# Second mixer: 35 elementwise instructions (product of y and gate, two running sums) moved from VectorE to GpSimd

## Chip, cores and metric

The kernel runs on one core of one Trainium2 chip. The metric is the device time of one execution in microseconds (us), lower is better. A profiled execution also gives a span, which is the time from its first to its last instruction.

## What is computed

The reference is two transformer-like blocks, one after the other, on 512 tokens of width 1024, in fp32. The change touches only the mixer of the second block, a convolution branch and a Mamba-2 branch (SSD):

```
u = a_half * sigmoid(b_half)
u = causal_depthwise_conv(u, conv_dw_w, conv_dw_b)      # 31 taps, 1024 channels
u = silu(layer_norm(u, conv_ln_w, conv_ln_b))           # mean and variance over the channels
...
y = ssd_chunked_scan(...) + d_skip * xs
y = y * silu(z)                                         # product of y and gate
yg = y.reshape(b, L, N_GROUPS, D_INNER // N_GROUPS)     # 4 groups of 512 channels
yg = yg * rsqrt(mean(yg * yg, axis=-1) + eps)           # sum of squares over a group
```

## The kernel before

Channels lie on the 128 partitions and the 512 tokens on the free axis, so that a tile is 128x512. A projection (`proj`) is 24 matmuls of 128x512 from weight blocks; every fp32 weight block is split into a high part by ScalarE (`whi`, line 201) and a low part by VectorE (`wlo`, line 203). The work is written as generators: `group_in` projects one group's tiles and, between projections, `pump` takes the next piece of two background queues. One holds the convolution (`conv31`, then `conv_sums`), the other the SSD of the group before (`ssd`). A scheduler then fixes one order for each engine; at run time every engine takes its instructions strictly in that order and waits on semaphores.

`conv31` makes 8 tiles of channels `co`, each by 30 multiply-adds on VectorE (line 1996, both tensor inputs in SBUF), and adds each finished tile to `self.sum` (`csum`, lines 2000 and 2002, seven adds). `conv_sums` starts with a matmul of `csum` (`pmean`, line 2025).

`ssd(g)` runs four times. Its last phase is a loop over i = 0 to 3, one tile of 128 channels each: TensorE makes `pyd` and `pyo` (line 2171), VectorE combines them into y (lines 2251, 2252, 2253), multiplies y by the gate z (line 2254), ScalarE squares y (lines 2257 and 2259), and VectorE adds the square into `ss` (tile `gsum`, line 2260; for i = 0 the square itself begins the sum). After the loop `col_sums` sums `gsum` over partitions with four small matmuls (`pms`, line 2010), VectorE scales them (`rg`, line 2016), GpSimd takes the power -1/2 (line 2017), and TensorE spreads the result over the partitions (`spread`, line 371), which VectorE multiplies into y (line 2270).

`decays` brings the decay tile `E` from DRAM by a transfer that GpSimd issues (line 2193). There are four `E` buffers, so the transfers of group g+1 are issued when the `pyd` matmuls of group g have freed them; they stand in GpSimd's queue between the end phases' steps. ScalarE's first operation on an `E` tile is line 2201.

Of the kernel before, what the change touches and what calls it, by code (L numbers as in the profile page):

```python
# [12 lines left out]
ALU = mybir.AluOpType  # L13
# [1903 lines left out]
class Mixer2:  # L1917
# [67 lines left out]
    def conv31(self):  # L1985

        K, nc = self.K, self.K.nc
        V, A = nc.vector, nc.scalar
        self.co = []
        self.sum = K.u(name="csum")  # L1990
        for i in range(8):
            u, c = self.uc[i], K.u(name="co")
            w = lambda j: K.cols["dw", j * 8 + i]
            A.activation(c, u[:, 0:512], AF.Identity, scale=w(0), bias=K.cols["db"][:, i:i + 1])
            for j in range(1, 31):
                V.scalar_tensor_tensor(c, u[:, j:j + 512], w(j), c, op0=ALU.mult, op1=ALU.add)  # L1996
                if j % 4 == 0:
                    yield
            if i == 1:
                V.tensor_tensor(self.sum, self.co[0], c, op=ALU.add)  # L2000
            elif i:
                V.tensor_tensor(self.sum, self.sum, c, op=ALU.add)
            self.co.append(c)
            yield

# [155 lines left out]
    def ssd(self, g, tiles):  # L2161

        K, nc = self.K, self.K.nc
        V, A, Te = nc.vector, nc.scalar, nc.tensor
        B, C, X, Z = tiles[0], tiles[1], tiles[2:6], tiles[6:10]
        ch = lambda x, c: x[:, c * 128:(c + 1) * 128]
        hs = slice(8 * g, 8 * g + 8)
        h8 = lambda x: x.rearrange("p (h j) -> p h j", j=64)
        bc = lambda x, c: x[:, c, hs, None].to_broadcast([128, 8, 64])
        def mul(*args, **kw):  # L2170
            self.line(lambda: Te.matmul(*args, start=True, stop=True, **kw))

        def turn(out, x):
            self.line(lambda: Te.transpose(out, x, K.ident))


        pbt = K.pt([128, 3, 128], name="pbt")
        for c in range(3):
            turn(pbt[:, c], ch(B, c))
        bt = K.u([128, 3, 128], name="btok")  # L2180
        A.activation(bt, pbt, AF.Copy)
        pcb = K.pt([128, 4, 128], name="pcb")
        for c in range(4):
            mul(pcb[:, c], ch(B, c), ch(C, c))
        cb = K.u([128, 4, 128], name="cbm")
        V.tensor_tensor(cb, pcb, self.tri[:, None, :].to_broadcast([128, 4, 128]), op=ALU.mult)
        Es, eas = [], []

        def decays(i):
            h0 = 8 * g + 2 * i  # L2190
            E = K.v4([128, 2, 4, 128], name="E")
            E2 = E.rearrange("p h c t -> p h (c t)")
            nc.gpsimd.dma_start(E2, self.acd[None, h0:h0 + 2, :].to_broadcast([128, 2, 512]))
            ea = K.u(name="ea")
            for hh in range(2):
                s = slice(hh * 64, hh * 64 + 64)
                A.activation(ea[s, 128:], E2[s, hh, 128:], AF.Exp)
            for hh in range(2):
                for c in range(4):
                    h = 2 * i + hh  # L2200
                    A.activation(E[:, hh, c], E[:, hh, c], AF.Relu, scale=-1.0,
                                 bias=self.acs[:, c, 8 * g + h:8 * g + h + 1])
            A.activation(E, E, AF.Exp, scale=-1.0)
            V.tensor_tensor(E, E, cb[:, None].to_broadcast([128, 2, 4, 128]), op=ALU.mult)
            Es.append(E)
            eas.append(ea)

        yield
        ps = [K.pt(name="pxT") for _ in range(4)]
        for c in range(4):  # L2210
            for i in range(4):
                turn(ps[c][:, i * 128:(i + 1) * 128], ch(X[i], c))
        xd, xws = [], []
        for c in range(4):
            x = K.u(name="xdt")
            V.tensor_tensor(h8(x), h8(ps[c]), bc(self.dt, c), op=ALU.mult)
            xd.append(x)
        for c in range(3):
            xw = K.u(name="xw")
            V.tensor_tensor(h8(xw), h8(xd[c]), bc(self.wd, c), op=ALU.mult)  # L2220
            xws.append(xw)
        decays(0)
        yield
        ps = [K.pt(name="pst") for _ in range(3)]
        for c in range(3):
            mul(ps[c], bt[:, c], xws[c])
        st = [None]
        for c in range(3):
            sn = K.u(name="st")
            if c == 0:  # L2230
                A.activation(sn, ps[c], AF.Copy)
            else:
                V.tensor_tensor(h8(sn), h8(st[c]), bc(self.et, c), op=ALU.mult)
                V.tensor_tensor(sn, sn, ps[c], op=ALU.add)
            st.append(sn)
        decays(1)
        yield
        for i in range(4):
            E, ea, z = Es[i], eas[i], Z[i]
            pd, po = K.pt(name="pyd"), K.pt(name="pyo")  # L2240

            for c in range(4):
                for hh in range(2):
                    h = 2 * i + hh
                    mul(pd[hh * 64:hh * 64 + 64, c * 128:(c + 1) * 128], xd[c][:, h * 64:h * 64 + 64], E[:, hh, c])
            for c in range(1, 4):
                mul(po[:, c * 128:(c + 1) * 128], st[c][:, i * 128:(i + 1) * 128], ch(C, c))
            if i < 2:
                decays(i + 2)
            y = X[i]  # L2250
            V.scalar_tensor_tensor(y, y, self.dsk[:, 4 * g + i:4 * g + i + 1], pd, op0=ALU.mult, op1=ALU.add)
            V.tensor_tensor(ea[:, 128:], po[:, 128:], ea[:, 128:], op=ALU.mult)
            V.tensor_tensor(y[:, 128:], y[:, 128:], ea[:, 128:], op=ALU.add)
            V.tensor_tensor(y, y, z, op=ALU.mult)
            if i == 0:
                ss = K.u(name="gsum")
                A.activation(ss, y, AF.Square)
            else:
                A.activation(z, y, AF.Square)
                V.tensor_tensor(ss, ss, z, op=ALU.add)  # L2260
            yield

        r = self.rsqrt4(self.rg[:, g], self.col_sums(ss), 512, 1e-6)
        yield
        yield
        rs = K.spread(r)
        for i in range(4):
            y = X[i]
            w = K.cols["sn"][:, 4 * g + i:4 * g + i + 1]
            V.scalar_tensor_tensor(y, y, w, rs, op0=ALU.mult, op1=ALU.mult)  # L2270
            self.y.append(y)
        yield
# [223 lines left out]
```

## Time and profile before

| what | value |
|---|---|
| median of 3 runs | 1889.6 us (1889.45 to 1890.53) |
| the profiled execution's own time | 1887.34 us |
| its span | 1885.6 us |
| TensorE busy | 1779.2 us, 94% of the span |
| VectorE busy | 1369.6 us, 73% |
| ScalarE busy | 943.3 us, 50% |
| GpSimd busy | 137.0 us, 7% |
| mean granted TensorE clock | 0.978 |

Busy shares are averages over stages of different kinds. The second mixer's groups run from about 985 to 1262 us of the span and the rest of its convolution until about 1400 us. PE is TensorE, DVE is VectorE, ACT is ScalarE and POOL is GpSimd. In a timeline row an entry with xN merges N neighbouring instructions.

### The profile page before, as it was taken

The page shows a single profiled execution, that of the slowest core. Times are in us where ns is not written, and L with a number is a line of the kernel's source. Part 1 is how long each engine was busy: PE and PEld are TensorE (multiplying, and loading weights), DVE is VectorE, ACT ScalarE, POOL GpSimd, SP SyncE. Part 2 cuts the span into 40 slices and gives each one's busy share as a digit, 9 for nine tenths or more (in the row PEclk, how much of TensorE's full clock was granted, in tenths as well). Part 3 has the DMA queues.
Part 4 walks back from the last instruction along what each step waited for, and adds up shares of the span by engine and source line. Part 5 has one row for each costly group of instructions (what it writes and reads, how often), then busy time and mean ns, then how long its engine had stood idle before and what let it go on. Part 6 is the DMA issues. An engine that isn't in the chain of part 4 may idle for free. (4 is left out here: it accounts for less than half of the span.)

```text
span 1885.6 us, 27902 instructions
## 1 busy us (share of the span) xinstructions
PE 1779.2 (94%) x10696; PEld 1481.2 (79%) x10696; DVE 1369.6 (73%) x2166; ACT 943.3 (50%) x1568; POOL 137.0 (7%) x247
## 2 busy tenths in 40 slices
PE   6998989998999998699999999999999999999997
PEld 3675878887888887478887777878778988788997
DVE  4888877867899997678969999999766753333324
ACT  5732355455888887442348577552253632223223
POOL 4000020121000000220000000000000100000000
PEclk9998989998999998899999999999999999999999
DMA  8732555535899999854433243344834753333334
GB/s 287 255 103 76 150 171 176 177 135 179 275 354 351 360 363 317 283 73 125 123 90 101 79 124 95 96 133 134 230 94 151 237 183 90 101 101 90 118 108 150
DMA packets 332905, 322.27 MB, mean 171 GB/s; under 512 B 16813, under 2 KB 291791, under 8 KB 332764
## 3 DMA queue, kind: packets, MB, share of 16 engines
q1 hardware_dynamic: 319004, 281.96, 47.7%
q0 software_dynamic: 11520, 35.30, 6.4%
q10 hardware_dynamic: 2240, 3.15, 0.5%
q8 instruction: 86, 1.41, 0.3%
q14 instruction: 55, 0.45, 0.1%
HBM read 299.03 MB, written 21.33 MB: 170 GB/s over the span
## 5 line engine op out<-in xcount | busy, mean ns | idle before, releaser
L201 ACT ACTIVATE whi<-wraw 128x1024 fp32r<-128x1024 f32 (+1 forms) x281 | 293.5, 1045 | 618.9 <-PE pin L237 209.8
L203 DVE TENSOR_TENSOR wlo<-wraw,whi 128x1024 fp32r<-128x1024 f32 (+1 forms) x281 | 337.9, 1203 | 210.9 <-ACT whi L201 208.5
L236 PE MATMUL pin<-hhi,whi 128*128 128x512 f32 (+1 forms) x752 | 306.4, 407 | 10.7 <-ACT sgc L2068 4.9
L238 PE MATMUL pin<-hhi,wlo 128*128 128x512 f32 (+1 forms) x752 | 300.3, 400 | 1.7 <-DVE wlo L203 1.7
L237 PE MATMUL pin<-hlo,whi 128*128 128x512 f32 (+1 forms) x752 | 300.7, 400 | 0.0
L236 PEld LDWEIGHTS pin<-hhi,whi 128*128 128x128 f32 (+1 forms) x752 | 141.3, 188 | 49.5 <-ACT sgc L2068 5.7
L1996 DVE SCALAR_TENSOR_TENSOR co<-uc,cols,co 128x512 f32<-128x512 f32 x240 | 176.9, 746 | 2.7
L238 PEld LDWEIGHTS pin<-hhi,wlo 128*128 128x128 f32 (+1 forms) x752 | 141.2, 188 | 39.0 <-DVE wlo L203 2.6
L237 PEld LDWEIGHTS pin<-hlo,whi 128*128 128x128 f32 (+1 forms) x752 | 141.2, 188 | 35.8 <-issue 2.4
L203 DVE TENSOR_TENSOR mwlo<-mwraw,mwhi 128x1024 fp32r<-128x1024 f32 x129 | 154.2, 1214 | 13.5 <-ACT mwhi L201 12.9
L201 ACT ACTIVATE mwhi<-mwraw 128x1024 fp32r<-128x1024 f32 x129 | 133.2, 1050 | 19.6 <-PE pgu L1723 8.2
L238 PE MATMUL pff<-hhi,wlo 128*128 128x512 f32 x336 | 133.0, 396 | 0.3 <-DVE wlo L203 0.3
L236 PE MATMUL pff<-hhi,whi 128*128 128x512 f32 x336 | 133.0, 396 | 0.0
L237 PE MATMUL pff<-hlo,whi 128*128 128x512 f32 x336 | 132.9, 396 | 0.0
L275 DVE SCALAR_TENSOR_TENSOR acc<-araw,silu,acc 128x1024 f32<-128x1024 f32 x70 | 89.7, 1281 | 29.8 <-DMA araw<-in_w_ada_ffn_dram 15.4
L1723 PE MATMUL pgu<-mwhi,xs 128*128 128x256 f32 x392 | 99.9, 290 | 8.3 <-DVEq L1764 8.2
L453 PE MATMUL pres<-wlo,fhi 128*128 128x256 f32 x352 | 97.4, 277 | 1.5 <-DVE wlo L203 1.5
L452 PE MATMUL pres<-whi,flo 128*128 128x256 f32 x352 | 97.2, 276 | 0.0
L450 PE MATMUL pres<-whi,fhi 128*128 128x256 f32 x352 | 97.2, 276 | 0.0
L1724 PE MATMUL pgu<-mwlo,xs 128*128 128x256 f32 x392 | 97.0, 284 | 0.0
L1723 PEld LDWEIGHTS pgu<-mwhi,xs 128*128 128x128 f32 x392 | 75.5, 193 | 8.8 <-issue 8.3
L1724 PEld LDWEIGHTS pgu<-mwlo,xs 128*128 128x128 f32 x392 | 75.4, 192 | 0.7 <-DVE mwlo L203 0.3
(631 smaller groups left out, 3848.1 us busy)
## 6 DMA issues: line engine op xcount, KB each, us to landing
wraw<-in_w_in_dram SPq DMA_DIRECT2D x98, 512.0 KB, 3.8
mwraw<-in_moe_w_up_dram SPq DMA_DIRECT2D x61, 512.0 KB, 7.2
araw<-in_ada_w_dram SPq DMA_DIRECT2D x48, 512.0 KB, 8.1
wraw<-in_w_ffn_in_dram SPq DMA_DIRECT2D x44, 512.0 KB, 3.7
mwraw<-in_moe_w_down_dram SPq DMA_DIRECT2D x33, 512.0 KB, 6.2
mwraw<-in_moe_w_gate_dram SPq DMA_DIRECT2D x33, 512.0 KB, 7.5
wraw<-in_moe_w_down_dram SPq DMA_DIRECT2D x31, 512.0 KB, 6.1
wraw<-in_moe_w_gate_dram SPq DMA_DIRECT2D x29, 512.0 KB, 5.7
```

The lines of the kernel that those rows point to most:

```text
L201: self.nc.scalar.activation(hi[:, :m], raw[:, :m], AF.Copy)
L203: self.nc.vector.tensor_tensor(lo[:, :m], raw[:, :m], hi[:, :m].bitcast(F32), op=ALU.subtract)
L236: t.matmul(out, lh, rh, start=start, stop=False)
L237: t.matmul(out, lh, rl, start=False, stop=False)
L238: return t.matmul(out, ll, rh, start=False, stop=stop)
L275: V.scalar_tensor_tensor(acc, raw[:, i], cs[:, q:q + 1], acc, op0=ALU.mult, op1=ALU.add)
L450: Te.matmul(o, yh[:, s], hi[:, k], start=(first and k == 0 and t == 0), stop=False, skip_group_check=True)
L452: Te.matmul(o, yl[:, s], hi[:, k], start=False, stop=False, skip_group_check=True)
L453: Te.matmul(o, yh[:, s], lo[:, k], start=False, stop=(last and k == kn - 1), skip_group_check=True)
L1723: Te.matmul(pg[:, j], x, hi[:, k], start=(kh == 0 and k == 0), stop=False)
L1724: Te.matmul(pg[:, j], x, lo[:, k], start=False, stop=(kh == 1 and k == 3))
L1996: V.scalar_tensor_tensor(c, u[:, j:j + 512], w(j), c, op0=ALU.mult, op1=ALU.add)
```

## The change

Three kinds of instruction are issued on GpSimd with the same operands: the product of y and z, the sum of a group's squares, and the sum of the convolution's tiles.

```diff
@@ conv31
             if i == 1:
-                V.tensor_tensor(self.sum, self.co[0], c, op=ALU.add)
+                nc.gpsimd.tensor_tensor(self.sum, self.co[0], c, op=ALU.add)
             elif i:
-                V.tensor_tensor(self.sum, self.sum, c, op=ALU.add)
+                nc.gpsimd.tensor_tensor(self.sum, self.sum, c, op=ALU.add)
@@ ssd
-            V.tensor_tensor(y, y, z, op=ALU.mult)
+
+            nc.gpsimd.tensor_tensor(y, y, z, op=ALU.mult)
             if i == 0:
                 ss = K.u(name="gsum")
                 A.activation(ss, y, AF.Square)
             else:
                 A.activation(z, y, AF.Square)
-                V.tensor_tensor(ss, ss, z, op=ALU.add)
+                nc.gpsimd.tensor_tensor(ss, ss, z, op=ALU.add)
```

The blank line shifts all later lines by one: the product is line 2255 in the changed kernel, the squares are 2258 and 2260, the sum is 2261.

The scheduler also orders the engines anew. On GpSimd, in the stretch from the first group's last phase (the fifth `E` transfer belongs to the second group):

```order
-L2193 DMA E<-acs_rows 128x1024 x8
+L2193 DMA E<-acs_rows 128x1024 x4
+L2000 TENSOR_TENSOR csum<-co 128x512
+L2002 TENSOR_TENSOR csum<-csum,co 128x512
+L2193 DMA E<-acs_rows 128x1024
+L2255 TENSOR_TENSOR xbc<-xbc,z 128x512
+L2193 DMA E<-acs_rows 128x1024
+L2255 TENSOR_TENSOR xbc<-xbc,z 128x512
+L2261 TENSOR_TENSOR gsum<-gsum,z 128x512
+L2193 DMA E<-acs_rows 128x1024
+L2255 TENSOR_TENSOR xbc<-xbc,z 128x512
+L2261 TENSOR_TENSOR gsum<-gsum,z 128x512
```

The transfers of the next group's `E`, which stood together, now alternate with the products (`xbc` is y) and the sums of the group that is ending.

On VectorE, at the end of the first group, from the last tile's line 2251 to the scaling of the column sums:

```order
 L2251 SCALAR_TENSOR_TENSOR xbc<-xbc,dsk,pyd 128x512
-L2260 TENSOR_TENSOR gsum<-gsum,z 128x512
 L2252 TENSOR_TENSOR ea<-pyo,ea 128x384
 L203 TENSOR_TENSOR wlo<-wraw,whi 128x1024
 L2253 TENSOR_TENSOR xbc<-xbc,ea 128x384
-L1996 SCALAR_TENSOR_TENSOR co<-uc,cols_11934,co 128x512
-L2254 TENSOR_TENSOR xbc<-xbc,z 128x512
-L1996 SCALAR_TENSOR_TENSOR co<-uc,cols_11934,co 128x512
-L2260 TENSOR_TENSOR gsum<-gsum,z 128x512
-L1996 SCALAR_TENSOR_TENSOR co<-uc,cols_11934,co 128x512
+L1996 SCALAR_TENSOR_TENSOR co<-uc,cols_11934,co 128x512 x5
 L2016 TENSOR_SCALAR rg<-pms 128x4
```

The product and the sums are gone and two further convolution steps have come ahead of line 2016; another five stand, in place of two, just before line 2251.

On TensorE, at the same place, around the column sums `pms`:

```order
 L237 MATMUL pin<-hlo,whi 128x512
 L238 MATMUL pin<-hhi,wlo 128x512
-L236 MATMUL pin<-hhi,whi 128x512
-L237 MATMUL pin<-hlo,whi 128x512
-L2010 MATMUL pms<-ones,gsum 128x1 x4
+L2010 MATMUL pms<-ones,gsum 128x1 x3
+L236 MATMUL pin<-hhi,whi 128x512
+L2010 MATMUL pms<-ones,gsum 128x1
+L237 MATMUL pin<-hlo,whi 128x512
 L238 MATMUL pin<-hhi,wlo 128x512
```

The column sums stand two projection matmuls earlier; so they do in the second and third group, and in the fourth they stand 13 matmuls (`pso`) earlier. TensorE's order is otherwise the same in the mixer, and the place of `pmean` too.

## Rows read from the trace of the kernel before

**Rows 1.** The page, busy time by engine.
```profile
PE 1779.2 (94%) x10696; PEld 1481.2 (79%) x10696; DVE 1369.6 (73%) x2166; ACT 943.3 (50%) x1568; POOL 137.0 (7%) x247
```
**Rows 2.** Busy time by stretch: columns window, us, PE, PEld, DVE, ACT, POOL, clock, DMA share, GB/s.
```profile
985.00:1340.00 355.00, 348.23 (x1786) 278.33 (x1785) 332.21 (x455) 203.49 (x346) 13.70 (x16) 1.00 0.40 116
```
**Rows 3.** TensorE's waits, 985 to 1340 us: total us, times, longest.
```profile
PE pyo L2171 <- DVE st L2234: 4.0, 3, 1.8
PE spread L371 <- POOL rg L2017: 0.9, 1, 0.9
PE pms L2010 <- DVE gsum L2260: 0.6, 1, 0.6
```
**Rows 4.** Instructions of a line or tile: ns min/median/max, first and last start.
```profile
L2254 DVE TENSOR_TENSOR xbc<-xbc,z x16: 678/682/691, 1017.1 to 1252.2; 128x512 f32<-128x512 f32 x16
...
L2260 DVE TENSOR_TENSOR gsum<-gsum,z x12: 680/689/693, 1029.1 to 1254.7; 128x512 f32<-128x512 f32 x12
...
L2002 DVE TENSOR_TENSOR csum<-csum,co x6: 682/684/691, 961.2 to 1333.8; 128x512 f32<-128x512 f32 x6
...
L2025 PE MATMUL pmean<-csum,mean x2: 590/590/591, 1361.5 to 1362.0; 128*128 128x512 f32 x2
```
**Rows 5.** GpSimd's groups of instructions: busy us, mean ns, idle before.
```profile
L534 POOL MEMSET lora<- 128x512 f32 x2 | 1.1, 532 | 0.1
...
L1931 POOL TENSOR_SCALAR_AFFINE_SELECT tri<-ones 128x128 f32<-128x128 f32 x1 | 0.3, 304 | 0.0
```
**Rows 6.** Timeline of VectorE at the first group's power: start us, length us.
```profile
1043.60 1.23 DVE L203 TENSOR_TENSOR wlo<-wraw,whi 128x1024 fp32r<-128x1024 f32 x1
1044.74 4.68 DVE L1996 SCALAR_TENSOR_TENSOR co<-uc,cols,co 128x512 f32<-128x512 f32 x6
```
**Rows 7.** Timeline of GpSimd: two powers, and an E transfer.
```profile
302.06 1.04 POOL L1086 TENSOR_TENSOR ml_sm<-ml_sm,mhalf 128x4 f32<-128x4 f32 x1 [11.75 <-DVE yr L797]
...
1043.76 1.95 POOL L2017 TENSOR_TENSOR rg<-rg,mhalf 128x4 f32<-128x4 f32 x1 [7.17 <-DVE rg L2016]
...
1108.08 0.53 POOL L2193 DMA_DIRECT2D E<-acs_rows  x1 [6.96 <-PE pyd L2171]
```
**Rows 8.** Timeline of VectorE: last tile's line 2251 in each group; 2253 in the second.
```profile
1035.81 0.75 DVE L2251 SCALAR_TENSOR_TENSOR xbc<-xbc,dsk,pyd 128x512 f32<-128x512 f32 x1 [0.54 <-PE pyd L2171]
...
1108.16 0.74 DVE L2251 SCALAR_TENSOR_TENSOR xbc<-xbc,dsk,pyd 128x512 f32<-128x512 f32 x1
...
1110.42 0.55 DVE L2253 TENSOR_TENSOR xbc<-xbc,ea 128x384 f32<-128x384 f32 x1
...
1181.57 0.75 DVE L2251 SCALAR_TENSOR_TENSOR xbc<-xbc,dsk,pyd 128x512 f32<-128x512 f32 x1 [0.50 <-PE pyd L2171]
...
1248.81 0.74 DVE L2251 SCALAR_TENSOR_TENSOR xbc<-xbc,dsk,pyd 128x512 f32<-128x512 f32 x1
```
**Rows 9.** Timeline of ScalarE: end of the second group.
```profile
1113.16 0.70 ACT L2201 ACTIVATE E<-E,ss_acs 128x128 f32<-128x128 f32 x2 [1.51 <-DMA E<-acs_rows]
1113.76 0.61 ACT L2259 ACTIVATE z<-xbc 128x512 f32<-128x512 f32 x1
```
**Rows 10.** Timeline of TensorE at the column sums of the four groups.
```profile
1042.07 0.39 PE L236 MATMUL pin<-hhi,whi 128*128 128x512 f32 x1
1042.30 0.39 PE L237 MATMUL pin<-hlo,whi 128*128 128x512 f32 x1
1042.53 0.95 PE L2010 MATMUL pms<-ones,gsum 128*128 128x1 f32 x8
...
1115.24 1.02 PE L2010 MATMUL pms<-ones,gsum 128*128 128x1 f32 x8 [0.56 <-DVE gsum L2260]
...
1188.29 0.95 PE L2010 MATMUL pms<-ones,gsum 128*128 128x1 f32 x8
...
1256.09 0.95 PE L2010 MATMUL pms<-ones,gsum 128*128 128x1 f32 x8
```

## Prediction

> **What bounds the kernel.** I read the page's busy times first: TensorE is busy 94% of the span and VectorE 73% [rows 1]. An average hides the stage that is changed, so the table by stretch comes next: from 985 to 1340 us TensorE is busy 348.2 of 355 us at full clock, and VectorE 332.2 [rows 2]. So in the second mixer TensorE leads, with 6.8 us of idle time in all, and VectorE follows closely, with 22.8 us. The list of waits then says what the 6.8 us are [rows 3]: 4.0 us for the state sums (three times), 0.9 us for one power on GpSimd, 0.6 us once for the sum of squares. This caps what a lighter VectorE can give: no more than those waits, about 5.5 us of 1887. The price of the change, in turn, can only be paid where TensorE stands waiting: its order is fixed, so a result that comes after the matmul that needs it costs its full lateness.
>
> **What is removed.** 16 products and 12 sums of squares leave VectorE, and seven sums of the convolution: six of line 2002 and one of line 2000 that I price alike [rows 4]. Each lasts 0.68 us, of which about 0.6 is taken from its neighbours, since VectorE's instructions overlap by some 0.09 us (1043.60 plus 1.23 is 1044.83, and the next starts at 1044.74 [rows 6]). 35 times 0.6 is 21 us of VectorE time. It is worth nothing by itself; only TensorE's waits for VectorE count. The waits for the state sums lie at the start of a group, not at its end, so I credit a third of the 4.0 us: **-1.3 us**. From below this credit is 0, from above the whole 5.5.
>
> **What is added.** 35 two-input instructions of 128x512 on GpSimd. The trace has none. From below, a memset of the same size, which reads nothing, takes 0.53 us; the nearest that reads is a select of 128x128 at 0.30 us [rows 5], which is 1.2 us for four times the columns; were each operand to cost that much, 2.4 us. I take 1.2, from the row that is nearest in kind (it reads, writes and computes), and keep 0.53 and 2.4 as ends. The Trainium skill (GPSIMD Engine Reference, section 3.1) gives 4497 ns for such an add with 2048 columns; a quarter is an estimate of 1.12 us, and the sum below would be 1.0 us lower by it. No run here shows it yet.
>
> GpSimd does not start at once. Its power of 128x4 took 1.04 us beside a VectorE that worked on small or PSUM operands, but 1.95 us when it started 0.16 us after line 203 had begun [rows 6, 7]: 0.9 us more, and line 203 had 1.07 us to go. So it waited for that VectorE instruction, whose two inputs are in SBUF. Most of VectorE's work here is of that kind (line 1996 above all, 0.78 us each [rows 6]), so behind an average one I add 0.35 us: 1.55 us from ready to done.
>
> **The chain at the end of a group.** Line 2251 of the last tile starts at S; line 2253 ends 2.81 us later (1108.16 to 1110.97 [rows 8]). Then come the product, 1.55, a square on ScalarE, 0.61 [rows 9], and the sum, 1.55; with 0.1 for the hand-overs the column sums can start at S + 6.6. TensorE reaches them, two matmuls of 0.23 us earlier than before [rows 10], at 1042.07, 1114.22 (1115.24 less its wait of 0.56 and the 0.46) and 1187.83, which is S + 6.3, + 6.1 and + 6.3.
> - First group: 0.35 us late. Third group: the same, 0.35.
> - Second group: ScalarE works in order, and the square stands behind an `E` tile that landed at 1113.16 [rows 9]. One step on it (0.35) and the square (0.61) end at 1114.15; plus 1.55 is 1115.7, late by 1.5 against 0.56 before: 0.9 more.
> - Fourth group: 13 matmuls earlier is 1253.1. With S at 1248.81 the sum comes at 1255.4; VectorE is 1.9 us behind TensorE there and can catch up as its products go, so 0.4 to 2.3; I take 1.0. The power behind it runs longer if it meets a 128x1024 instruction, as in the first group: 0.5 more.
>
> That is **+3.1 us**.
>
> **What GpSimd takes from VectorE.** If GpSimd has to wait until a VectorE instruction is over, they share something, and I expect VectorE to wait for GpSimd in turn, for the 1.2 us that the new instructions run. The trace cannot show this: the powers read four columns, and the six steps beside one of them took 0.78 us each, as elsewhere. In each group's last round one product and one sum run between line 2253 of tile 2 and line 2251 of tile 3, where the new order has four to six steps of line 1996 on VectorE. Two holds of 1.2 us, less the two instructions of 0.6 that are gone, make S 1.2 us later: four groups, **+4.8 us**. The Trainium skill (SBUF — State Buffer, section Who interferes with whom) says that a VectorE instruction with two SBUF inputs contends with a GpSimd instruction that reads SBUF, and that the second to come blocks fully; the trace agrees for GpSimd's side, with 1.95 against 1.04 us, and no run here shows the other side. By the row alone, with GpSimd waiting only, this term is 0 (first rival).
>
> **Costed at nothing.** The seven sums of the convolution: the last ends by 1334.5, and `pmean` runs at 1361.5 in an unmoved place [rows 4], so 27 us cover them. The `E` transfers now queue behind products and sums on GpSimd; the last of a group is issued when `pyd` frees its buffer (1108.08 [rows 7]), and ScalarE gets it 5.1 us later [rows 9]. The sum ahead of it is done by then if each new instruction keeps to 1.55 us; if not, up to one of them (1.55) times three groups, 4.7 us, comes on top, as ScalarE's square would wait with it. No step on SP's queue moves.
>
> **Sum.** 3.1 + 4.8 - 1.3 = 6.6 us. The profiled execution took 1887.34 us, so 1893.9 in its terms; the median of the runs is 2.3 us above it, so **1896.2 us**.
>
> **Rivals.**
> - *One-sided waiting.* VectorE never waits for GpSimd; then 3.1 - 1.3 = +1.8, 1891.4 us. For it: the undisturbed steps of line 1996 [rows 6]; against it: those powers hardly read anything. 23%.
> - *Relief wins (the other side: faster).* The new instructions take under about 0.9 us, the chain closes before TensorE arrives (S + 5.3 instead of 6.6), and VectorE, 21 us lighter, is early for all three waits: -5.5, 1884.1 us. It decides at 1.4 us from ready to done. For it: the memset's 0.53 us; against: a memset reads no input. 12%.
> - *VectorE becomes the bound.* 35 holds of 1.2 us take 42 us and 21 are saved. Of the 21 left over VectorE's 22.8 us of idle time can take half, as the rest is waiting for TensorE, ScalarE and DMA that stays; 10.5 us more reach TensorE through late `wlo` tiles: 1906.7 us. 10%.
> - That the change does not do what it says is excluded by the order of the engines.
>
> **Numbers.** My forecast has 55%; its own range is 1892 to 1903 us. Within 0.2%, about 3.8 us, a measurement of this kernel cannot tell it from no change, which is up to 1893.4: the first rival's 23% and 5% of the forecast's. So faster 12%, same 28%, slower 60%. The range runs from 1886 to 1905: it leaves out most of the relief case and of the bound case, and it takes in prices from 0.7 to 1.9 us for a GpSimd instruction; 0.53 and 2.4 us lie outside with those two cases.
>
> **What would show it.** Line 2255 and 2261 at 1.2 to 1.9 us on GpSimd; TensorE's waits for the column sums (`pms` for GpSimd's `gsum`) at about 7 us in four waits, longest in the second or fourth group; steps of line 1996 beside a GpSimd product with a start delayed by about 1.2 us; waits for the state sums little changed; the time after 1340 us the same length as before. If `pms` waits stay under 2 us in all, the forecast is wrong; if VectorE's steps keep their 0.78 us spacing beside the products, the term of 4.8 us falls.

## The result, and the profile after

The changed kernel takes 1913.7 us (median of 1907.4 to 1914.7), the kernel before, timed beside it, 1890.1: 1.0113 times the time, 95% interval 1.0090 to 1.0137. Slower was right, but the time lies outside the range (1886 to 1905). The profiled execution took 1907.4 us against 1887.3, so 20 us are there to be found; executions of one kernel differ by up to 14 us, the longer ones at a lower granted clock (the kernel before: 1887.3 us at 0.978, 1898.3 at 0.973), so small differences below are read from the profiles. The profiled execution is the fastest of the changed kernel's four: the other three took 1913 to 1915 us, at a clock of 0.971 to 0.972 against 0.975.

The page of the changed kernel, busy time by engine, against [rows 1]:

```profile
PE 1785.7 (94%) x10696; PEld 1485.9 (78%) x10696; DVE 1375.5 (72%) x2131; ACT 940.5 (49%) x1566; POOL 193.9 (10%) x282
```

VectorE has 35 instructions less and 5.9 us more to do. Nothing was taken off it.

The same work in both kernels lies between the first group's `pbt` on TensorE and `pmean`. The table by stretch of it, for the kernel before and for the changed one (columns as in [rows 2]):

```profile
987.00:1361.50 374.50, 367.73 (x1869) 294.22 (x1868) 341.75 (x463) 206.92 (x349) 13.70 (x16) 1.00 0.42 122
```
```profile
986.00:1380.30 394.30, 375.15 (x1870) 298.94 (x1869) 347.62 (x430) 204.51 (x348) 67.87 (x49) 0.98 0.40 116
```

All 19.8 us arise here; what follows `pmean` is as long as before (524.1 and 525.0 us to the end of the span). On TensorE they split in two: its idle time grows from 6.8 to 19.2 us (12.4), and the same 1869 matmuls take 375.2 instead of 367.7 us (7.4), at a granted clock of 0.98 instead of 1.00. In three pieces, 13.6 us together, the granted clock was 1.2 instead of 2.4 GHz; half of that, 6.8 us, is nearly all of the 7.4.

TensorE's waits in the changed kernel in that stretch, against [rows 3]:

```profile
PE pms L2010 <- POOL gsum L2261: 10.8, 4, 4.6
PE pyo L2171 <- DVE st L2234: 4.0, 3, 1.8
PE pin L238 <- DVE wlo L203: 2.5, 1, 2.5
PE pyd L2171 <- issue: 1.1, 1, 1.1
PE pin L236 <- ACT whi L201: 0.5, 1, 0.5
```

The column sums are waited for in every group (3.26, 1.88, 1.04 and 4.59 us), the state sums exactly as before, and a wait for `wlo` is new.

**GpSimd and VectorE hold each other.** The instructions of line 2255 on GpSimd, and the groups of line 1996 on VectorE from 985 to 1340 us, changed and before:

```profile
L2255 POOL TENSOR_TENSOR xbc<-xbc,z x16: 1274/1717/2754, 1015.4 to 1265.8; 128x512 f32<-128x512 f32 x16
```
```profile
L1996 DVE SCALAR_TENSOR_TENSOR co<-uc,cols,co 128x512 f32<-128x512 f32 x144 | 123.3, 871 | 1.8
```
```profile
L1996 DVE SCALAR_TENSOR_TENSOR co<-uc,cols,co 128x512 f32<-128x512 f32 x149 | 109.0, 747 | 1.3
```

A mean step of line 1996 grew from 747 to 871 ns: 144 times 124 ns is 17.9 us. Counted one by one, 28 of the 430 VectorE instructions of the stretch last over 0.15 us longer than such an instruction did before, 0.92 us in the median and 24.8 us together; 21 of them are steps of line 1996. Singly it looks like this at the end of the fourth group, VectorE first, then GpSimd (start us, length us):

```profile
1265.18 0.54 DVE L2253 TENSOR_TENSOR xbc<-xbc,ea 128x384 f32<-128x384 f32 x1
1265.65 0.74 DVE L1996 SCALAR_TENSOR_TENSOR co<-uc,cols,co 128x512 f32<-128x512 f32 x1
1266.31 2.28 DVE L275 SCALAR_TENSOR_TENSOR acc<-araw,silu,acc 128x1024 f32<-128x1024 f32 x1
1268.51 1.75 DVE L1996 SCALAR_TENSOR_TENSOR co<-uc,cols,co 128x512 f32<-128x512 f32 x1
```
```profile
1265.80 1.70 POOL L2255 TENSOR_TENSOR xbc<-xbc,z 128x512 f32<-128x512 f32 x1 [3.96 <-DVE xbc L2253]
1268.25 1.47 POOL L2261 TENSOR_TENSOR gsum<-gsum,z 128x512 f32<-128x512 f32 x1 [0.74 <-ACT z L2260]
```

The product is ready at 1265.80, while a step of line 1996 runs to 1266.39; it lasts 1.70 us instead of the least 1.27, so it waited for most of what the step had left. Line 275, 1.28 us in the kernel before, starts behind it and lasts 2.28: it waited 1.0 us for the product. The next step lasts 1.75 instead of 0.74 behind the sum. The hold does not show as a late start but as a longer instruction. This is the side that no run had shown; it agrees with the Trainium skill (SBUF — State Buffer, section Who interferes with whom), by which the second to come blocks fully. The figure of the Trainium skill for the length (GPSIMD Engine Reference, section 3.1; the estimate of 1.12 us from it) is near the 1.27 us measured where nothing was in the way.

**The clock falls behind a wait.** TensorE at the end of the fourth group:

```profile
1264.78 0.40 PE L238 MATMUL pin<-hhi,wlo 128*128 128x512 f32 x1
1269.77 1.27 PE L2010 MATMUL pms<-ones,gsum 128*128 128x1 f32 x8 [4.59 <-POOL gsum L2261]
1270.90 0.77 PE L236 MATMUL pso<-yhi,whi 128*128 128x512 f32 x1
1271.47 0.63 PE L237 MATMUL pso<-ylo,whi 128*128 128x512 f32 x1
1271.90 0.63 PE L238 MATMUL pso<-yhi,wlo 128*128 128x512 f32 x1
```

Before the wait matmuls follow each other every 0.23 us, behind it every 0.43 us: 1.2 instead of 2.4 GHz. The same stands behind the wait of 3.26 us (0.63 us each from 1046.67 on) and behind the one for `wlo` of 2.47 (from 1185.20 on), and not behind those of 1.88 and 1.04 us. My sum had no term for it.

### The profile page after: what moved, and what is told of

It reads as the page before. It is cut to its first block, busy times and chain, and to the rows that moved or that the text cites. A ratio compares the mean times of both kernels' runs of the same rounds, so it can differ in the third digit from the quotient of the medians.

```text
span 1905.3 us, 27923 instructions
## 1 busy us (share of the span) xinstructions
PE 1785.7 (94%) x10696; PEld 1485.9 (78%) x10696; DVE 1375.5 (72%) x2131; ACT 940.5 (49%) x1566; POOL 193.9 (10%) x282
## 5 line engine op out<-in xcount | busy, mean ns | idle before, releaser
L1996 DVE SCALAR_TENSOR_TENSOR co<-uc,cols,co 128x512 f32<-128x512 f32 x240 | 194.9, 821 | 3.3
L236 PEld LDWEIGHTS pin<-hhi,whi 128*128 128x128 f32 (+1 forms) x752 | 142.1, 189 | 50.7 <-ACT sgc L2068 5.7
L275 DVE SCALAR_TENSOR_TENSOR acc<-araw,silu,acc 128x1024 f32<-128x1024 f32 x70 | 93.7, 1339 | 27.7 <-DMA araw<-in_w_ada_ffn_dram 15.4
```

Of the source, the lines that this page charges most:

```text
L236: t.matmul(out, lh, rh, start=start, stop=False)
L275: V.scalar_tensor_tensor(acc, raw[:, i], cs[:, q:q + 1], acc, op0=ALU.mult, op1=ALU.add)
```

## Experiments

Two theories were set against each other. *Late column sums*: the loss lies at the ends of the groups, where a longer chain meets a fixed place in TensorE's order. *VectorE too full*: VectorE is late everywhere because it is held, and the lateness comes out wherever TensorE next needs it. The table gives each run's ratio to the kernel before on the same chip, and of its profile the stretch from `pbt` to `pmean` as TensorE's busy and idle time, with its waits for `pms` and `spread` together.

| run | ratio (95% interval) | stretch = busy + idle, us | pms + spread |
|---|---|---|---|
| before | | 374.5 = 367.7 + 6.8 | 1.5 |
| changed | 1.0113 (1.0090 to 1.0137) | 394.3 = 375.2 + 19.2 | 10.8 |
| e_prod | 1.0038 (1.0026 to 1.0050) | 384.1 = 373.2 + 10.9 | 3.2 |
| e_sum | 1.0053 (1.0036 to 1.0070) | 392.0 = 378.8 + 13.2 | 8.1 |
| e_conv | 1.0005 (0.9992 to 1.0018) | 378.1 = 369.7 + 8.4 | 0.9 |
| e_hold | 1.0041 (1.0028 to 1.0054) | 383.3 = 373.0 + 10.3 | 5.1 |
| e_gw3 | 1.0043 (1.0025 to 1.0062) | 385.4 = 374.4 + 11.0 | 5.2 |
| e_relief | 0.9974 (0.9958 to 0.9991) | 373.0 = 367.8 + 5.2 | 0 |
| e_late1 | 1.0113 (1.0089 to 1.0137) | 405.6 = 381.5 + 24.1 | 15.5 |
| b_late1 | 1.0015 (0.9999 to 1.0031) | 380.2 = 369.8 + 10.4 | 5.1 |
| e_both | 1.0095 (1.0071 to 1.0119) | 394.8 = 375.1 + 19.7 | 12.4 |
| b_both | 1.0007 (0.9996 to 1.0018) | 378.1 = 369.8 + 8.3 | 0.5 |
| e_last_both | 1.0079 (1.0059 to 1.0099) | 391.5 = 376.2 + 15.3 | 6.0 |
| e_both2 | 1.0099 (1.0069 to 1.0130) | 394.1 = 375.8 + 18.3 | 4.6 |
| b_both2 | 0.9997 (0.9979 to 1.0016) | 378.2 = 369.5 + 8.7 | 0.9 |
| e_three | 1.0046 (1.0027 to 1.0065) | 386.2 = 372.4 + 13.8 | 0 |
| e_two | 1.0041 (1.0024 to 1.0058) | 382.9 = 371.7 + 11.2 | 0.9 |

The profiles of e_sum and e_late1 are executions 10 and 9 us above the median of their runs, that of the changed kernel is 6 us below; waits can be read from them, totals less so. The scheduler orders the engines anew for each run; no run holds the order fixed.

### The three parts alone

e_prod changes the first of these lines only, e_sum the second, e_conv the last two:

```diff
-            V.tensor_tensor(y, y, z, op=ALU.mult)
+            nc.gpsimd.tensor_tensor(y, y, z, op=ALU.mult)
...
-                V.tensor_tensor(ss, ss, z, op=ALU.add)
+                nc.gpsimd.tensor_tensor(ss, ss, z, op=ALU.add)
...
-                V.tensor_tensor(self.sum, self.co[0], c, op=ALU.add)
+                nc.gpsimd.tensor_tensor(self.sum, self.co[0], c, op=ALU.add)
...
-                V.tensor_tensor(self.sum, self.sum, c, op=ALU.add)
+                nc.gpsimd.tensor_tensor(self.sum, self.sum, c, op=ALU.add)
```

> Only the 16 products go to GpSimd; sums of squares and of the convolution stay on VectorE. Theory 'late column sums' (TensorE waits at pms because the group's last chain is longer and VectorE reaches it late, and then runs at the lower clock for some us): one instruction of the chain is 1.0 us longer and about one hold of 1.05 us less 0.6 falls ahead of it, so the pms waits come to 5 to 6 us against 10.8, the clock costs about 3 us, 1898 to 1901 us. Theory 'VectorE too full' (every hold reaches TensorE through late wlo tiles): 16 of 33 holds, half of 24 us, 1902 us, with waits for wlo rather than for pms.

> Only the 12 sums of squares go to GpSimd. 'Late column sums': again one instruction of the last chain is 1.0 us longer, and of the holds only one lies ahead of the last tile in each group; ScalarE no longer waits for a product. pms waits of 5 to 6 us, 1897 to 1900 us. 'VectorE too full': 12 of 33 holds, 1899 us, in waits for wlo. A rival of its own, 'ScalarE stalls at the squares' (they wait 19.3 us for GpSimd's products in the changed kernel and make whi and E late): nothing of that is left here, so it expects 1892 us.

> Only the seven sums of the convolution go to GpSimd, none of which lies in a chain that TensorE waits for. 'Late column sums': 1890 us, plus or minus 2. 'VectorE too full': seven holds of 1.05 less 0.6 saved is 3 us, 1893 us. Each hold should be seen: a step of line 1996 of about 1.79 instead of 0.74 us beside each sum.

Measured: 1898.4, 1900.6 and 1892.0 us beside a before of 1890.9. The excesses, 0.38, 0.53 and 0.05%, add up to 0.96% of the 1.13%; none of the three parts gives anything back. e_conv shows that the seven sums far from the chain cost nothing that can be measured; the steps of 1.79 us that were expected beside each sum did not come (three VectorE instructions of the stretch are longer, none of them of line 1996, by 2.3 us together), and its interval does not tell 1890 from 1893 us. In e_prod the waits for `pms` are 2.8 us, half of what the first theory expected, 2.6 us are waits for `wlo` and `whi`, as the second expects, and the matmuls take 5.5 us more: the size of the time fits the first theory, its make-up fits neither. e_sum's waits for `pms`, 7.7 us in its profile, are more than expected; without any product on GpSimd it costs at least as much as e_prod, so ScalarE's stalls at the squares are not needed for the cost.

e_prod also shows which VectorE instruction is held. VectorE and GpSimd at the second tile's product:

```profile
1025.90 0.73 DVE L2100 SCALAR_TENSOR_TENSOR xbc<-pin,cols,xbc 128x511 f32<-128x511 f32 x1
1026.68 1.76 DVE L203 TENSOR_TENSOR wlo<-wraw,whi 128x1024 fp32r<-128x1024 f32 x1
```
```profile
1026.07 1.30 POOL L2254 TENSOR_TENSOR xbc<-xbc,z 128x512 f32<-128x512 f32 x1 [3.81 <-DVE xbc L2253]
```

Line 2100 reads `pin` from PSUM; the product starts beside it and needs no more than 1.30 us, and line 2100 no more than its 0.73. Line 203, whose two inputs are in SBUF, comes next and lasts 1.76 us instead of 1.22.

### The hold alone

```diff
             V.tensor_tensor(y, y, z, op=ALU.mult)
+            nc.gpsimd.tensor_tensor(scr, y, y, op=ALU.mult)
...
                 V.tensor_tensor(ss, ss, z, op=ALU.add)
+                nc.gpsimd.tensor_tensor(scr, ss, ss, op=ALU.add)
```

> The kernel before, with VectorE doing all of its work, and besides 16 products and 12 sums on GpSimd (same size, two SBUF inputs) whose result nobody uses: no chain is longer by an instruction, only the holds are there. If GpSimd holds VectorE up, line 1996 lasts 1.05 us longer beside each of them, 28 holds, 29 us of VectorE time, more than its 22.8 us of idle time in the stretch: pms waits of 2 us a group from the holds ahead of it, then the clock, 1902 to 1915 us. If the hold were one-sided or only a matter of how spans are recorded: 1890 us.

Measured: 1898.1 us, ratio 1.0041. Work on GpSimd whose result nobody uses costs 7 us, so one-sided waiting falls. The size stayed under the expectation: the stretch has 8.0 us more of VectorE's busy time (349.8 against 341.8), not 29. Only 15 VectorE instructions are longer by over 0.15 us, by 9.3 us together; five of them are the sums of squares themselves. Reading one tile twice, the added instructions need only 1.03 us at least. TensorE waits 3.6 us for `pms` and 1.5 for `spread`, and 5.3 us lie in slower matmuls.

### The wait alone

```diff
+        for _ in range(3):
+            nc.gpsimd.tensor_tensor(ss[:, 0:4], ss[:, 0:4], K.ones[:, 0:4], op=ALU.mult)
         r = self.rsqrt4(self.rg[:, g], self.col_sums(ss), 512, 1e-6)
```

> The kernel before, with three small GpSimd multiplications (128x4, by one) between a group's last sum and its column sums: the chain is some 3 us longer, VectorE's work is all as before and hardly anything holds it. If a TensorE wait costs more than its length because the clock is lower behind it: four waits of 2.5 us or so, 10 us, and 5 to 7 us of slower matmuls, 1905 to 1908 us. If the slow stretches of the changed kernel have another cause (VectorE, power of GpSimd's work): waits alone, 1900 us, granted clock 1.00 behind them.

Measured: 1900.3 us, ratio 1.0043. TensorE's waits in its profile:

```profile
PE pms L2010 <- POOL gsum L2264: 5.2, 4, 2.5
PE pyo L2171 <- DVE st L2234: 3.9, 3, 1.7
PE pyd L2171 <- issue: 1.1, 1, 1.1
PE pso L237 <- DVE ylo L232: 0.7, 1, 0.7
```

and the table of its stretch:

```profile
988.10:1373.50 385.40, 374.38 (x1869) 298.77 (x1868) 343.09 (x463) 207.21 (x349) 19.09 (x28) 0.98 0.41 119
```

The waits came out half as long as I expected, 4.2 us more of idle time, and VectorE's work is unchanged but for 1.3 us, with no instruction over 0.15 us longer than before; yet the matmuls take 6.7 us longer. The time is that of the other expectation, 1900 us, but by chance: that one had waits alone and a granted clock of 1.00, and here it is 0.98. A wait of TensorE can cost more than its length. In the other runs with longer waits, e_sum and e_late1 aside, the matmuls' part is 0.6 (changed kernel) to 1.5 times (e_hold) the added idle time; some 2 us of it are within what profiles differ by, since e_conv and the controls b_late1, b_both and b_both2 have 369.5 to 369.8 us of busy time too. In e_conv and b_both the matmuls are slower behind a wait of 1.8 us for the state sums that the kernel before has as well, at full clock. This is the term that the prediction lacked; twelve GpSimd operations of 128x4 are all that it took here.

### Relief alone

This run leaves out the products of the first three tiles and the sums of the second and third in each group:

```diff
-            V.tensor_tensor(y, y, z, op=ALU.mult)
+            if i == 3:
+                V.tensor_tensor(y, y, z, op=ALU.mult)
...
-                V.tensor_tensor(ss, ss, z, op=ALU.add)
+                if i == 3:
+                    V.tensor_tensor(ss, ss, z, op=ALU.add)
```

> The kernel before, leaving out the products of the first three tiles and the sums of the second and third in each group, so VectorE has 20 instructions less and GpSimd none more: what a lighter VectorE alone gives. The prediction credited 1.3 us, with 5.5 as the bound. TensorE's waits for the state sums (4.0) should tell: if they are VectorE's lag they shrink, 1885 to 1888 us; if they are the length of their own chain they stay and nothing is gained, 1889 to 1891 us.

Measured: ratio 0.9974, 1888.6 beside 1893.2 us. What is won in the profiled stretch, 1.5 us, is the waits for `pms` and `spread`; those for the state sums stay at 4.0 us, so they are not VectorE's lag. The medians differ by 4.7 us, more than the stretch shows; the profile of the kernel before is one of its faster executions. The prediction's credit of 1.3 us was put on the wrong waits and was no overstatement, but it needs a VectorE that really is lighter.

### Room behind the last tile

e_late1 and b_late1 (the changed kernel, and the control from the kernel before):

```diff
+        yield
         r = self.rsqrt4(self.rg[:, g], self.col_sums(ss), 512, 1e-6)
```

> The changed kernel with one more step of the generator ahead of the column sums: in the first three groups pms stands 22 to 24 matmuls (some 5 us) later in TensorE's order, in the fourth its place is the same. 'Late column sums': the waits of 3.3, 1.9 and 1.0 us go, with the slow stretch behind the first; the fourth group's 4.6 us and the slow stretch behind it stay. 6 us of waits and some 3 us of clock come back: about 1904 us, pms waits about 4.6. 'VectorE too full': the same time is lost in other waits (wlo, spread), 1910 us or more.

> The kernel before with the same step: the control for the run above. Its pms waits are 0.6 us in all, so both theories expect no change, 1888 to 1892 us.

Measured: 1916.8 us, as without the step, and 1895.8 beside 1893.2 for the control. e_late1's waits:

```profile
PE spread L371 <- POOL rg L2017: 10.8, 3, 5.8
PE pms L2010 <- POOL gsum L2261: 4.7, 1, 4.7
PE pyo L2171 <- DVE st L2234: 4.0, 3, 1.8
PE pin L238 <- DVE wlo L203: 3.6, 1, 3.6
```

Only the fourth group still waits at `pms`; the others wait at the next place of the same chain, the spread, which had hardly moved (in the first group it stands 3 places later in TensorE's order, with `pms` 24 places later). Even the control waits 5.1 us there. This told nothing yet between the theories, so the spread was moved as well.

```diff
+        if g < 3:
+            yield
         r = self.rsqrt4(self.rg[:, g], self.col_sums(ss), 512, 1e-6)
...
+        if g < 3:
+            self.scale = scale
+            return
...
         yield
+        if g:
+            self.scale()
+            yield
         ps = [K.pt(name="pxT") for _ in range(4)]
```

`scale` holds the spread and the four scalings; it runs in the next group. e_both does this to the changed kernel, b_both to the kernel before, e_last_both to the changed kernel with the fourth tile's product and sum on VectorE; in e_three, below, the condition is `g == 3`:

```diff
-            nc.gpsimd.tensor_tensor(y, y, z, op=ALU.mult)
+            G = V if i == 3 else nc.gpsimd
+            G.tensor_tensor(y, y, z, op=ALU.mult)
...
-                nc.gpsimd.tensor_tensor(ss, ss, z, op=ALU.add)
+                G.tensor_tensor(ss, ss, z, op=ALU.add)
```

> The changed kernel with both TensorE places that hang on the group's last chain put later: the column sums by 24 matmuls and the spread of their root into the next group (some 80 matmuls later); in the fourth group the sums stand 16 matmuls later too. The earlier run that put only pms later lost the same time at the spread. 'Late column sums': waits for pms and spread fall from 10.8 to under 2 us, the slow stretches behind them go, and what stays is the wait for wlo (2.5) and a slow stretch behind that: 1892 to 1898 us. 'VectorE too full': VectorE is behind all along, so the waits turn up at wlo, pyd and the state sums: 1905 us or more.

> The kernel before with the same two places put later: the control, and the candidate for a version faster than both. Its waits for pms and spread in the mixer are 1.5 us, so 'late column sums' expects 1 to 3 us less than before, 1887 to 1891 us by the runs of before seen first; 'VectorE too full' expects no difference.

> As e_both, but the fourth tile's product and sum are back on VectorE, so GpSimd has 12 products, 8 sums and the convolution's seven. 'Late column sums': no wait left that e_both has not lost, and a chain that is 2 us shorter: as e_both or up to 2 us less. 'VectorE too full': 8 of the 35 holds less, 1902 us.

Measured: 1908.8, 1892.4 and 1905.8 us beside 1890.6. The `yield` behind `self.scale()` had moved the second and third group's own last tiles by the same 24 matmuls, so only the first group had room. e_last_both came out 3.0 us below e_both, between the two expectations (up to 2, and 7). Without that one `yield`:

> The earlier run e_both put a step into the generator that moved the whole of the second and third group as well, so their column sums stood no later behind the last tile than before (24 matmuls), and their waits stayed (12.4 us in three); only the first group's, which did stand 24 matmuls later, had none. Here that step is taken out: in the first three groups the column sums stand 48 matmuls behind the last tile and the spread in the next group; the fourth group is as in the changed kernel. 'Late column sums': no pms or spread wait in the first three groups, about 4.6 us in the fourth with its slow stretch, 1898 to 1902 us. 'VectorE too full': other waits (wlo, pyd, state sums) take their place, 1908 us or more.

> As e_both2, with the fourth group's products and sums back on VectorE: 12 products, 9 sums and the convolution's seven stay on GpSimd, and no group has its column sums late. 'Late column sums': pms and spread waits under 1.5 us in all, no slow stretch at a group's end, 1890 to 1894 us. 'VectorE too full': 28 of 35 holds are there, so about 28/35 of 18 us stay, 1904 us.

> The kernel before with the same two moves as e_both2 and e_three, all of its work on VectorE: the control for them. In those two, waits have come up at the start of the fourth group (pst for xw 3.4, whi 2.6, wlo 1.8 us and a slow stretch) where the scalings now stand ahead of xw on VectorE. If the holds make VectorE late there, this run has none of them and stays at 1889 to 1893 us. If the move itself does it, they are here too, with 1898 to 1900 us, and then e_three owes nothing to the holds.

Measured: e_both2 1910.9 beside 1890.7, e_three 1900.8, and the control b_both2 1895.3 beside 1892.3 (0.9997). e_both2's waits, in the whole stretch, and those of e_three:

```profile
PE pms L2010 <- POOL gsum L2263: 4.3, 1, 4.3
PE pst L2171 <- DVE xw L2222: 4.0, 2, 3.4
PE pyd L2171 <- issue: 3.6, 2, 2.5
PE pin L236 <- ACT whi L201: 2.6, 1, 2.6
PE pin L238 <- DVE wlo L203: 2.2, 2, 1.8
```
```profile
PE pst L2171 <- DVE xw L2222: 4.0, 2, 3.4
PE pyd L2171 <- issue: 3.6, 2, 2.5
PE pin L236 <- ACT whi L201: 2.6, 1, 2.6
PE pin L238 <- DVE wlo L203: 2.2, 2, 1.9
PE pyo L2171 <- DVE st L2236: 1.3, 1, 1.3
```

The first three groups' waits for `pms` are gone, 6.2 us of them, and other waits have come in their place; the time stayed. That is what *VectorE too full* said, but not all of them need be VectorE's lag: the control b_both2 has 5.0 us of waits at `pyd`, against 3.6. e_three came out between the two expectations, 1890 to 1894 and 1904 us, nearer to the second. Without the fourth group's late sums it wins back 8 us of e_both2's stretch (4.3 of wait, 0.3 at the spread, 3.4 of busy time behind it), and loses the rest at the places above. In the control, with the same moves and no GpSimd work, the wait of `pst` for `xw` is 1.1 us in all.

The table by stretch shows how long room helps. The changed kernel and e_both2, the first two groups and then the third:

```profile
985.00:1131.00 146.00, 137.57 (x725) 108.97 (x725) 135.28 (x175) 94.70 (x167) 31.02 (x25) 0.99 0.33 96
1131.00:1204.00 73.00, 67.16 (x347) 52.51 (x346) 65.32 (x81) 46.63 (x82) 17.34 (x13) 0.98 0.34 95
```
```profile
985.00:1131.00 146.00, 142.57 (x751) 113.04 (x750) 138.16 (x175) 94.73 (x168) 33.97 (x25) 1.00 0.35 101
1131.00:1204.00 73.00, 65.18 (x339) 51.22 (x338) 65.48 (x83) 45.21 (x81) 14.78 (x12) 0.95 0.33 92
```

For 146 us TensorE is as busy as in the kernel before (142.1), and then the third group gives the gain back. One more run asked whether that is the third group's own doing, with `G` as VectorE from the third group on:

```diff
-            G = V if g == 3 else nc.gpsimd
+            G = V if g >= 2 else nc.gpsimd
```

> As e_three, with the third group's products and sums back on VectorE too: 8 products, 6 sums and the convolution's seven stay on GpSimd. In e_three the first two groups lost nothing (TensorE busy 142.6 of 146 us, as before the change), and all that was left to lose came up between the third group's last tiles and the fourth's start (whi, wlo, xw). If these come from VectorE and ScalarE being late in that group, they go: 1890 to 1893 us, with the first two groups still at about 142.6. If the holds cost in proportion wherever they are: 21 of 35 instructions, about half of the 21 us, 1900 us.

Measured: 1898.8 us, ratio 1.0041; the expectation of 1890 to 1893 missed. The other expectation, a cost in proportion to the instructions moved, had 1900. The waits for `whi` and `wlo` shrink (to 0.7 and 0.9 us), but the longest wait is the same as in e_three, `pst` for `xw`, 3.4 us, and it lies at the start of the third group (the expectations call it the fourth's), at 1151 us, before any of its products. VectorE was late there: until 1135.21 us ScalarE had waited 6.63 us for its line 2100. Then VectorE itself stood idle twice, waiting for ScalarE, just ahead of the first scaling (line 2275):

```profile
1136.62 0.75 DVE L2100 SCALAR_TENSOR_TENSOR xbc<-pin,cols,xbc 128x509 f32<-128x509 f32 x1 [1.50 <-ACT xbc L2097]
1142.12 1.23 DVE L203 TENSOR_TENSOR wlo<-wraw,whi 128x1024 fp32r<-128x1024 f32 x1 [1.71 <-ACT whi L201]
1143.92 0.74 DVE L2275 SCALAR_TENSOR_TENSOR xbc<-xbc,cols,spread 128x512 f32<-128x512 f32 x1
```

No run separates how much of the wait for `xw` comes from the holds of the two groups before, from the new order of VectorE and ScalarE, and from the four scalings moved ahead of `xw`. In b_both2, without any hold, `pst` waits at most 0.5 us, but `pyd` in the same group waits 2.7.

No version with the same result beats the kernel before: b_both and b_both2 cannot be told from it, and e_relief leaves work out.

## Why the prediction was wrong

Term by term, in us of the profiled execution:

| term | predicted | measured |
|---|---|---|
| waits for `pms`, beyond before | 7.4 (3.1 + 4.8, less 0.5 for the power) | 10.2 |
| power and spread | 0.5 | -0.9 |
| state sums (relief) | -1.3 | 0 |
| `wlo` and `whi` | 0 | 3.1 |
| the same matmuls at a lower clock | no term | 7.4 |
| sum | 6.6 | 19.8 |

**The step that failed first** is "the price of the change, in turn, can only be paid where TensorE stands waiting", where a late result "costs its full lateness". 12.4 of the 19.8 us were paid so. The other 7.4 were paid behind the waits, by the same matmuls at 1.2 GHz, and the sum had no term for it; e_gw3 shows such a loss behind added waits alone, of the order of the waits themselves. It is the largest single part of the 13 us missed in the profile, even less the 2 us by which profiles differ. By the medians the miss is 17.5 us: the profiled execution is 6.3 us below the median, where the prediction took 2.3.

**The second** is that holds outside the last round were left out, as if VectorE's idle time would take them. Its busy time in the stretch grew by 5.9 us with 33 instructions less; at the 0.6 us each by which the prediction priced them the holds took some 25.7 us, 0.78 each, and the longer instructions counted one by one give 24.8. In the changed kernel the lag comes out as 3.1 us of waits at `wlo` and `whi`. This is the rival "VectorE becomes the bound", given 10% and 1906.7 us. It counted 21 us of extra VectorE time where there are 6, and lacked the clock; of the rivals it came nearest.

**The length** was near: 1.27 us undisturbed against 1.2, a median of 1.72 with the waiting inside against 1.55. The chain from line 2251 to the column sums took 6.9 to 7.1 us, predicted 6.6; in the second group too, where the prediction had the square stand behind an `E` tile.

**The hold** was foreseen and is 1.0 us instead of 1.2. Whether it makes S, the start of the last tile's line 2251, later by 1.2 us in each group shows in the time from S to TensorE's arrival at `pms`, which is the start of `pms` less its wait:

```profile
1037.40 0.74 DVE L2251 SCALAR_TENSOR_TENSOR xbc<-xbc,dsk,pyd 128x512 f32<-128x512 f32 x1
1113.12 0.74 DVE L2251 SCALAR_TENSOR_TENSOR xbc<-xbc,dsk,pyd 128x512 f32<-128x512 f32 x1
1192.46 0.74 DVE L2251 SCALAR_TENSOR_TENSOR xbc<-xbc,dsk,pyd 128x512 f32<-128x512 f32 x1
1262.92 0.73 DVE L2251 SCALAR_TENSOR_TENSOR xbc<-xbc,dsk,pyd 128x512 f32<-128x512 f32 x1
```
```profile
1044.51 0.87 PE L2010 MATMUL pms<-ones,gsum 128*128 128x1 f32 x6 [3.26 <-POOL gsum L2261]
1120.26 0.83 PE L2010 MATMUL pms<-ones,gsum 128*128 128x1 f32 x6 [1.88 <-POOL gsum L2261]
1199.60 0.61 PE L2010 MATMUL pms<-ones,gsum 128*128 128x1 f32 x4 [1.04 <-POOL gsum L2261]
```

| group | S to arrival, without a hold (prediction) | measured | S later by |
|---|---|---|---|
| 1 | 6.3 | 3.9 | 2.4 |
| 2 | 6.1 | 5.3 | 0.8 |
| 3 | 6.3 | 6.1 | 0.2 |
| 4 | 4.3 | 2.3 | 2.0 |

The total, 5.4 us against 4.8, is near, but by luck: it is about two whole holds in the first and the fourth group and hardly any in the third. In the first, as the order showed, convolution steps filled the place of the two instructions that are gone; in the fourth, line 275 at 2.29 and line 1996 at 1.79 us stand just ahead of line 2251. Some 8 us before S in the third, TensorE had itself waited 3.0 us for `whi` and `wlo`, which may be why S is hardly late there; no run tests it. In the fourth group VectorE did not catch up, for which the prediction had taken off 1.3 us, but fell further behind; with `pms` 13 matmuls earlier, the wait became 4.6 us. These 1.3 us, 0.9 of longer chains and 0.6 of hold are the 2.8 us by which the waits for `pms` were missed.

**At nothing:** rightly so for the convolution's sums (e_conv) and for the time behind 1340 us. The `E` transfers brought no wait of TensorE for them in the list above.

**The other rivals:** one-sided waiting is refuted by e_hold and by the single instructions; relief falls by its own condition, 1.4 us from ready to done, since the product alone takes 1.72 in the median, and VectorE did not become lighter. Where VectorE really has 20 instructions less (e_relief), it gives a quarter of a per cent, about what that rival forecast.

What is shown: the mutual hold, its size, that added waits cost clock besides, and that room behind the last tile alone recovers nothing clear of the intervals. Not shown is why the slow stretch follows some waits of 1.2 to 1.9 us and not others (in e_gw3 one begins some 2 us behind the third wait, 1.30 us, and none behind the fourth, 1.20), nor how much of the lateness at `whi`, `wlo` and `xw` is the scheduler's new order.

## What to carry to other kernels

Moving a two-input elementwise instruction from VectorE to GpSimd took no load off VectorE here, while both read SBUF: each held VectorE about 0.78 us on average and saved some 0.6. Read VectorE's mean per instruction by line before and after, since the hold hides inside longer instructions and not in the list of waits. Where TensorE is the bound, price each new wait at more than its length (1.6 times in the changed kernel, 2.6 times in e_gw3), and ask where a late engine's lag comes out next before giving one place more room.

## What the runs showed of the hardware that was not expected

- A held VectorE instruction starts on time and lasts longer (line 1996 at 1.75 to 1.79 instead of 0.74 us); with one input in PSUM it is not held (line 2100, six times beside a product or sum on GpSimd in the changed kernel, never over 0.75 us; line 2252 of e_hold, which is line 2251 of the kernel before, seven times, never over 0.75 us).
- GpSimd's add or product of 128x512 takes 1.27 us undisturbed with two tiles, 1.03 us when both inputs are the same tile.
- The profiles have 20 waits of TensorE of 2.5 us and more in the stretch. The granted clock fell to 1.2 GHz during 18 of them or within 2.3 us behind; it stayed at 2.4 GHz behind 3.37 us at `pst` in e_both2 and 2.52 us at `pyd` in e_three. In e_gw3 it fell also right behind a wait of 1.70 us for the state sums (the matmuls are slower from 1166.39 us on), and in e_conv and b_both behind the same wait of 1.80 to 1.81, while the kernel before kept 2.4 GHz behind it, at 1.81 us.
